# Scores of the two later query blocks as unpadded 64-row products of both halves in turn, in a hybrid encoder layer

## The chip, the cores and the metric

The kernel runs on one core of one Trainium2 chip. The metric is the device time of one execution in microseconds (us). Lower is better.

## What is computed

One layer of an encoder for 512 positions of width 1024. It has three parts in a row, each added to its input: a mixer (pooling, a recurrent time mixer called RWKV-7, and differential attention side by side, then an output projection), a cross-attention into 256 memory rows, and a gated feed-forward part. The change touches the differential attention alone. Cut to that:

```python
q, k, v = jnp.split(z, 3, axis=-1)                     # 4 heads, 2 halves of 64 features
q = rms_normalize(q.reshape(B, S, H, 2, 64)) * q_norm
k = rms_normalize(k.reshape(B, S, H, 2, 64)) * k_norm
def block(q_blk, start):                               # 4 blocks of 128 queries
    s = einsum('bqhcd,bkhcd->bhcqk', q_blk, k) * scale # a score matrix for each half c
    s = where(visible, s - slope * abs(qpos - kpos), -inf)
    p = softmax(s)
    p = p[:, :, 0] - lam * p[:, :, 1]
    return einsum('bhqk,bkhd->bqhd', p, v)
```

## The kernel before

Every large product is made of three products in a reduced float format (fp32r): each operand is held as a high part and a low part, and `mm3` (lines 330 to 333) adds high x high, high x low and low x high into one PSUM tile. So a product of `mm3` shows in a profile as one row each of L331, L332 and L333. Products that are not split (transposes with the identity, the small products of the recurrence) run in plain float32; each of them shows as two matmul records.

The program is written as a list of steps. A string, `MIX`, names the order of the steps of the mixer, and a scheduler that works with a timeline of its own decides the final order on each engine. It prefers what it takes to be ready first. So two products that stand next to each other in the source need not stand next to each other on TensorE.

The differential attention has the steps `q` (transposes of queries and keys of a head into `qk` and `qz`), `s` (`diff_s(h, i)`: scores and softmax of head `h`, query block `i`), `o` (`diff_o`: transposes `pT` and products with the values) and `n` (`diff_norm`). Because a block sees no later keys, block `i` needs `n = 128 (i + 1)` keys: 128, 256, 384 and 512 columns. A head has two halves `c` of 64 features. They lie in partitions 0 to 63 and 64 to 127 of `qk`. Before the change a half is picked out by padding: the stationary operand `qz[c]` holds the queries of half `c` in its 64 rows and zeros in the other 64 (lines 713 to 717), and the product runs over all 128 rows. In each block half 0 has its three products, then half 1. Its score tiles `S` come from the PSUM buffers `pr` for head 0 and `b` for the other heads, two buffers each. VectorE reduces a score tile with the bias (L750), and so frees it; ScalarE takes the exponential.

The kernel already has products over 64 rows elsewhere, in plain float32. The products `ua` (L476) and `uw` (L487) use one half of the rows. The products `T` (L575) use rows 0 to 63 for one PSUM tile and rows 64 to 127 for another. In the first quarter of `T` the scheduler put the two tiles one after the other; in the second they stand in turn (`T_706`, `T_707`, `T_706`, `T_707`, ...); in the third they begin with two of the same tile (`T_734`, `T_734`, `T_735`, `T_735`, then in turn). Other engines that the prediction speaks of: `ss` (L788, a column sum in `diff_norm`), the powers on GpSimd (`s_r` L680, `m_rstd` L402), and the recurrence of `chunk` (products `U` L905 and `S` L916, and the VectorE addition `r` L907).

Of the kernel before, what the change touches and what calls it, by code (L numbers as in the profile page):

```python
# [16 lines left out]
P = 128  # L17
S = 512
# [175 lines left out]
def trunk_body(ctx: ExitStack, tc: tile.TileContext, A):  # L194
# [11 lines left out]
    def slot(tag, bufs, shape=(P, 512), dt=F32, nm=None):  # L206
        cnt[0] += 1
        pool = keep if tag in ("d", "t", "r", "rb") else sb
        return pool.tile(list(shape), dt, name=f"{nm or tag}_{cnt[0]}", tag=tag, bufs=bufs)
# [10 lines left out]
    def rs(dt=F32, shape=(P, 512)):  # L220
        return slot("r", TB["r"], shape, dt)

    def ts(dt=F32, shape=(P, 512)):
        return slot("t", TB["t"], shape, dt)
# [7 lines left out]
    def kvs(dt=F32, shape=(P, 512)):  # L232
        return slot("kv", TB["kv"], shape, dt)

    def small(role, shape, bufs=4):
        return slot("s_" + role, bufs, shape)

    def ps(tag, nm=None):
        cnt[0] += 1
        if tag in ("a0", "a1"):  # L240
            return pp.tile([P, 512], F32, name=f"{nm or 'ps'}_{cnt[0]}", tag=tag, bufs=1)
        return pp.tile([P, 512], F32, name=f"{nm or 'ps'}_{cnt[0]}", tag=tag, bufs=2)

    def pr(nm=None):
        return ps("pr", nm)
# [5 lines left out]
    V, G, ACT, PE = nc.vector, nc.gpsimd, nc.scalar, nc.tensor  # L251
    mm = PE.matmul
# [72 lines left out]
    def act_el(*a, **k):  # L325

        with tc.issue_after(pre_el[0]):
            el_ins.append(ACT.activation(*a, **k).ins)

    def mm3(out, lh, ll, rh, rl, start, stop):  # L330
        mm(out, lh, rh, start=start, stop=False)  # L331
        mm(out, lh, rl, start=False, stop=False)  # L332
        mm(out, ll, rh, start=False, stop=stop)  # L333
# [139 lines left out]
    for p in range(2):  # L473
# [3 lines left out]
        a = rs()  # L477
# [6 lines left out]
    for p in range(2):  # L484
# [3 lines left out]
        s = kvs()  # L488
# [114 lines left out]
    for q in range(4):  # L603
        pt = pr("W0")
        p4 = pt.rearrange("p (c h v) -> p c h v", c=2, h=4)
        for c in range(2):
            for h in range(H):
                mm(p4[0:64, c, h, :], tav(2 * q + c, h)[64:128], AV[q][64:128, c, h, :],  # L608
                   start=True, stop=True)
# [84 lines left out]
    bias = slot("bias", 1)  # L694
# [11 lines left out]
    for h in range(H):  # L706
# [6 lines left out]
    qz = [[sb.tile([P, 512], F32R, name=f"qz{c}{i}", tag=f"qz{c}{i}", bufs=1) for i in range(2)]  # L713
          for c in range(2)]
# [24 lines left out]
    def diff_s(h, i):  # L739

        qk = qks[h]
        n = P * (i + 1)
        nmx, Z, rz = small("nmx", (P, 2)), small("Z", (P, 2)), small("rz", (P, 2))
        sc = []
        for c in range(2):
            st = pr("S") if h == 0 else ps("b", "S")
            qs = slice(i * P, (i + 1) * P)
            mm3(st[:, 0:n], qz[c][0][:, qs], qz[c][1][:, qs], qk[0][:, 0:n], qk[1][:, 0:n], True, True)
            s = ts()
            V.tensor_tensor_reduce(s[:, 0:n], st[:, 0:n], bias[:, 384 - P * i:S],  # L750
                                   -(0.25 ** (h + 1)), 3e38, ALU.add, ALU.min, nmx[:, c:c + 1])
            sc.append(s)
        for c in range(2):
            act_el(sc[c][:, 0:n], sc[c][:, 0:n], AF.Exp, scale=-1.0, bias=nmx[:, c:c + 1],
                   accum_out=Z[:, c:c + 1])
        V.reciprocal(rz, Z)
        V.tensor_scalar(rz[:, 1:2], rz[:, 1:2], lam, None, ALU.mult)
        if i >= 2:
            ACT.activation(sc[1][:, 0:n], sc[1][:, 0:n], AF.Copy, scale=rz[:, 1:2])
        else:  # L760
            V.tensor_scalar(sc[1][:, 0:n], sc[1][:, 0:n], rz[:, 1:2], None, ALU.mult)
        V.scalar_tensor_tensor(sc[0][:, 0:n], sc[0][:, 0:n], rz[:, 0:1], sc[1][:, 0:n],  # L762
                               ALU.mult, ALU.subtract)
        sc0[h, i] = sc[0]
# [275 lines left out]
    def v_rows(h):  # L1040
# [20 lines left out]
        "e": [lambda h=h: k_t(h) for h in range(H)],  # L1061
        "q": [lambda h=h: qks.update({h: qk_t(h)}) for h in range(H)],
        "s": [lambda h=h, i=i: diff_s(h, i) for h in range(H) for i in range(4)],
        "o": [lambda h=h, b=b: diff_o(h, *b) for h in range(H) for b in (((0, 1), (0, 1)), ((2, 3), (0, 1)), ((2, 3), (2, 3)))],
        "n": [lambda h=h: diff_norm(h) for h in range(H)],
# [52 lines left out]
    on, KT, Vm, qs, qr = {}, {}, {}, {}, {}  # L1118
# [354 lines left out]
```

## Time and profile before

| | us |
|---|---|
| median of 3 runs | 800.82 (800.76 to 801.9) |
| the profiled execution, its own time | 800.4 |
| its span, first to last instruction | 798.6 |
| TensorE busy in it | 785.8 (98%) |
| VectorE busy | 560.3 (70%) |
| ScalarE busy | 420.7 (53%) |

An engine's busy time is the time in which at least one of its instructions runs. Matmuls are pipelined, so their durations overlap: what one costs TensorE is read from the distance of two starts, not from its duration. The time outside the span (1.8 us) is start and end of the program.

### The profile page before, as it was taken

The numbers are of one execution on the slowest core, as the hardware profiler recorded it, in microseconds if no ns is written. First come the engines' busy times: TensorE is split into PE (matmuls) and PEld (weight loads), VectorE is DVE, ScalarE is ACT, GpSimd is POOL, SyncE is SP. The second block draws the span as 40 slices with busy tenths as digits, with TensorE's granted clock in tenths as the row PEclk, the third lists the DMA queues.
The fourth block names the chain that finished last, engine by engine and source line by source line (L and its number), as shares of the span: only waits on it lengthen the run. The fifth ranks groups of instructions, "written<-read, shape, count | busy, mean of one in ns | idle before, by whom it ended". The sixth has DMA issues, their size and how long they took to land.

```text
span 798.6 us, 11546 instructions
## 1 busy us (share of the span) xinstructions
PE 785.8 (98%) x4130; PEld 654.3 (82%) x4130; DVE 560.3 (70%) x1075; ACT 420.7 (53%) x778; POOL 64.0 (8%) x83
## 2 busy tenths in 40 slices
PE   8999999989899999999999999999999999999997
PEld 6867788879798888888888888888888888888886
DVE  6558668856798855756646576666666667898995
ACT  7364643576689854556545344444334344454662
POOL 3010400243600000000100000000000000000000
PEclk9999999989999999999999999999999999999999
DMA  7312113222021244221112322232222323534432
GB/s 268 132 67 92 67 54 132 80 81 80 27 92 57 79 149 154 93 81 66 40 66 80 123 90 100 86 103 93 93 96 89 106 93 124 183 115 131 132 94 79
DMA packets 43625, 79.22 MB, mean 99 GB/s; under 512 B 4784, under 2 KB 5936, under 8 KB 43568
## 3 DMA queue, kind: packets, MB, share of 16 engines
q1 hardware_dynamic: 41328, 75.35, 27.9%
q10 hardware_dynamic: 2240, 3.15, 1.2%
q8 instruction: 32, 0.52, 0.3%
q14 instruction: 25, 0.20, 0.1%
HBM read 76.38 MB, written 2.10 MB: 98 GB/s over the span
## 4 chain that ended last, share of the span: by engine, by line
PE 95%; ACT 1%; POOL 1%; issue 1%; DVE 1%; DMA 1%; DVEq 0%; SPq 0%; ACTq 0%
PE ps L331 23%; PE ps L333 22%; PE ps L332 22%; PE ps L1406 13%; POOL s_r L680 1%; PE T L575 1%; PE tr L523 1%; PE colsum L393 1%; PE S L332 1%; PE S L331 1%; PE S L333 1%; PE pT L775 1%; DMA wr<-in_wp_dram 1%; PE Sx L331 1%; PE W L608 1%
## 5 line engine op out<-in xcount | busy, mean ns | idle before, releaser
L174 ACT ACTIVATE wh<-wr 128x512 fp32r<-128x512 f32 x212 | 132.4, 628 | 159.3 <-PE ps L332 121.2
L175 DVE TENSOR_TENSOR wl<-wr,wh 128x512 fp32r<-128x512 f32 x212 | 146.0, 690 | 97.1 <-ACT wh L174 92.9
L331 PE MATMUL ps<-r,wh 128*128 128x512 f32 x416 | 162.3, 394 | 0.0
L332 PE MATMUL ps<-r,wh 128*128 128x512 f32 x416 | 162.0, 389 | 0.0
L333 PE MATMUL ps<-r,wl 128*128 128x512 f32 x416 | 161.2, 390 | 0.0
L333 PEld LDWEIGHTS ps<-r,wl 128*128 128x128 f32 x416 | 78.1, 188 | 16.5
L331 PEld LDWEIGHTS ps<-r,wh 128*128 128x128 f32 x416 | 78.1, 188 | 16.3 <-ACT r L312 0.2
L332 PEld LDWEIGHTS ps<-r,wh 128*128 128x128 f32 x416 | 78.2, 188 | 16.3 <-DVE t L762 0.2
L1406 PE MATMUL ps<-whid,ma 128*128 128x512 f32 x276 | 85.3, 389 | 0.0
L331 PE MATMUL ps<-wh,xh 128*128 128x256 f32 (+1 forms) x224 | 75.3, 336 | 0.2 <-ACT kv L1014 0.2
L332 PE MATMUL ps<-wl,xh 128*128 128x256 f32 (+1 forms) x224 | 74.9, 334 | 0.0
L1406 PEld LDWEIGHTS ps<-whid,ma 128*128 128x128 f32 x276 | 51.7, 188 | 11.2 <-ACT whid L312 0.5
L1406 PE MATMUL ps<-wlod,ma 128*128 128x512 f32 x138 | 53.4, 389 | 0.0
L312 ACT ACTIVATE whid<-r 128x512 fp32r<-128x512 f32 x55 | 34.3, 630 | 30.1 <-PE ps L1406 20.1
L1353 DVE TENSOR_TENSOR t<-ps,rb 128x512 f32<-128x512 f32 x44 | 29.4, 686 | 27.4 <-PE ps L333 27.0
L331 PEld LDWEIGHTS ps<-wh,xh 128*128 128x128 f32 x224 | 42.4, 189 | 5.4 <-issue 0.7
L332 PEld LDWEIGHTS ps<-wl,xh 128*128 128x128 f32 x224 | 42.5, 190 | 4.5 <-issue 0.7
L332 PE MATMUL ps<-xl,wh 128*128 128x512 f32 x112 | 44.2, 399 | 0.0
L313 DVE TENSOR_TENSOR wlod<-r,whid 128x512 fp32r<-128x512 f32 x55 | 36.8, 682 | 4.4 <-ACT whid L312 4.3
L332 PE MATMUL ps<-d,wh 128*128 128x512 f32 x96 | 37.7, 392 | 0.0
L333 PE MATMUL ps<-wh,xl 128*128 128x512 f32 x96 | 37.6, 393 | 0.0
L333 PE MATMUL ps<-d,wl 128*128 128x512 f32 x96 | 37.5, 390 | 0.0
(343 smaller groups left out, 1470.2 us busy)
## 6 DMA issues: line engine op xcount, KB each, us to landing
wr<-in_wp_dram SPq DMA_DIRECT2D x212, 256.0 KB, 2.6
r<-in_wd_dram SPq DMA_DIRECT2D x33, 256.0 KB, 2.7
wrawd<-in_wd_dram SPq DMA_DIRECT2D x22, 256.0 KB, 2.7
r<-in_xt_dram SPq DMA_DIRECT2D x8, 256.0 KB, 5.3
t<-in_xt_dram ACTq DMA_DIRECT2D x8, 256.0 KB, 2.7
out_dram<-t SPq DMA_DIRECT2D x8, 256.0 KB, 2.0
kv<-in_memt_dram ACTq DMA_DIRECT2D x4, 256.0 KB, 4.4
pm<-in_pmat_dram SPq DMA_DIRECT2D x1, 512.0 KB, 4.0
```

Source lines behind the costliest of these rows:

```text
L174: nc.scalar.activation(hi, raw, AF.Copy)
L175: nc.vector.tensor_tensor(lo, raw, hi.bitcast(F32), ALU.subtract)
L312: ins = ACT.activation(dhi, src, AF.Copy)
L313: V.tensor_tensor(dlo, src, dhi.bitcast(F32), ALU.subtract)
L331: mm(out, lh, rh, start=start, stop=False)
L332: mm(out, lh, rl, start=False, stop=False)
L333: mm(out, ll, rh, start=False, stop=stop)
L393: mm(pt[:, 2 * i:2 * i + 2], tot[:, i * P:(i + 1) * P], ones[:, 0:2], start=True, stop=True)
L523: PE.transpose(pv4[0:n, c, p, :], src(p, 2 * q + c), ident)
L575: mm(pts[hh].rearrange("p (c h t) -> p c h t", c=2, h=2)[:, c, p], KB[p][o:o + 64, cg, :], RA[p][o:o + 64, cg, :], start=True, stop=True)
L1353: V.tensor_tensor(dst[c], src[c], rb2, ALU.mult)
L1406: mm(X[p][tt], l, r, start=not onto and k == 0 and j == 0, stop=k == NG - 1 and j == 2, skip_group_check=onto)
```

## The change

For the blocks `i` = 2 and 3 of each head the padding is no longer multiplied. Half 0 uses rows 0 to 63 of both operands, half 1 rows 64 to 127. The source issues the six products of a block in turn: high x high of half 0, of half 1, then high x low of half 0, of half 1, then low x high. Both score tiles are taken before the first product. The zeros are still written, since blocks 0 and 1 still use them.

```diff
-        sc = []
+        sc, sts = [], [pr("S") if h == 0 else ps("b", "S") for _ in range(2)]
+        qs = slice(i * P, (i + 1) * P)
+        if i < 2:
+            for c in range(2):
+                mm3(sts[c][:, 0:n], qz[c][0][:, qs], qz[c][1][:, qs], qk[0][:, 0:n], qk[1][:, 0:n],
+                    True, True)
+        else:
+            for j, (a, b) in enumerate(((0, 0), (0, 1), (1, 0))):
+                for c in range(2):
+                    rows = slice(64 * c, 64 * c + 64)
+                    mm(sts[c][:, 0:n], qz[c][a][rows, qs], qk[b][rows, 0:n], start=j == 0, stop=j == 2)
         for c in range(2):
-            st = pr("S") if h == 0 else ps("b", "S")
-            qs = slice(i * P, (i + 1) * P)
-            mm3(st[:, 0:n], qz[c][0][:, qs], qz[c][1][:, qs], qk[0][:, 0:n], qk[1][:, 0:n], True, True)
             s = ts()
-            V.tensor_tensor_reduce(s[:, 0:n], st[:, 0:n], bias[:, 384 - P * i:S],
+            V.tensor_tensor_reduce(s[:, 0:n], sts[c][:, 0:n], bias[:, 384 - P * i:S],
```

The scheduler makes a new order of TensorE from it. These are three of the eight blocks. In the rows, `qz_866` and `qz_867` are the high and low part of half 0, `qz_868` and `qz_869` those of half 1; `ps` are products with weights, `pT` and `kT` transposes, `U`, `S_2055` and `y` products of the recurrence.

Head 1, block 2, on TensorE before:

```order
L905 MATMUL U_2049<-b_2036,at 128x128 x2
L1034 MATMUL kT_2590<-cs,kv_2152 128x128 x4
L331 MATMUL S_2237<-d_2075,qz_866 128x384
L332 MATMUL S_2237<-d_2076,qz_866 128x384
L333 MATMUL S_2237<-d_2075,qz_867 128x384
L331 MATMUL S_2243<-d_2075,qz_868 128x384
L332 MATMUL S_2243<-d_2076,qz_868 128x384
L333 MATMUL S_2243<-d_2075,qz_869 128x384
```

The same block in the changed kernel:

```order
L331 MATMUL ps_2630<-wh_1_2316,xh_1889 128x256
L754 MATMUL S_2237<-d_2075,qz_866 128x384
L754 MATMUL S_2237<-d_2076,qz_866 128x384
L754 MATMUL S_2237<-d_2075,qz_867 128x384
L754 MATMUL S_2238<-d_2075,qz_868 128x384
L754 MATMUL S_2238<-d_2076,qz_868 128x384
L754 MATMUL S_2238<-d_2075,qz_869 128x384
L923 MATMUL S_2055<-r_598,r_751 128x128 x2
```

The six products still stand side by side, but three of half 0 come first and then three of half 1. They moved behind a group of weight products.

Head 2, block 3, on TensorE before; the three products of its second half stand 23 rows further on, also side by side:

```order
L331 MATMUL o_2408<-p_2449,d_1300 128x256
L331 MATMUL S_2723<-d_2382,qz_866 128x512
L332 MATMUL S_2723<-d_2383,qz_866 128x512
L333 MATMUL S_2723<-d_2382,qz_867 128x512
L931 MATMUL y_2212<-r_774,r_599 128x128
```

The first half of this block in the changed kernel; its second half stands 10 rows further on, between weight products and the product `gnv`:

```order
L952 MATMUL gnm_2255<-r_1631,cs 128x512
L754 MATMUL S_2723<-d_2382,qz_866 128x512
L754 MATMUL S_2723<-d_2383,qz_866 128x512
L782 MATMUL pT_2599<-cs,t_2470 128x128 x2
L754 MATMUL S_2723<-d_2382,qz_867 128x512
L726 MATMUL qkT_2741<-cs,d_1937 128x128
```

The three products of one half are now in two pieces, with transposes over 128 rows between them.

Head 3, block 3, on TensorE before:

```order
L331 MATMUL ps_3248<-r_3002,wh_0_2964 128x512
L331 MATMUL S_3125<-d_2755,qz_866 128x512
L332 MATMUL S_3125<-d_2756,qz_866 128x512
L333 MATMUL S_3125<-d_2755,qz_867 128x512
L331 MATMUL S_3131<-d_2755,qz_868 128x512
L332 MATMUL S_3131<-d_2756,qz_868 128x512
L333 MATMUL S_3131<-d_2755,qz_869 128x512
L332 MATMUL ps_3248<-r_3003,wh_0_2964 128x512
```

The same block in the changed kernel:

```order
L333 MATMUL ps_3027<-wh_1_2934,xh_2021 128x256
L754 MATMUL S_3125<-d_2755,qz_866 128x512
L754 MATMUL S_3126<-d_2755,qz_868 128x512
L754 MATMUL S_3125<-d_2756,qz_866 128x512
L754 MATMUL S_3126<-d_2756,qz_868 128x512
L754 MATMUL S_3125<-d_2755,qz_867 128x512
L754 MATMUL S_3126<-d_2755,qz_869 128x512
L782 MATMUL pT_3144<-cs,t_2881 128x128
```

This is the one block of the eight in which the halves stand in turn. Around all of them rows of other steps changed places too, from the transposes of head 0 on to the first weight products of the output projection; behind these the order of TensorE is as before.

## Rows read from the trace of the kernel before

**Rows 1.** The page's first part: busy us (share of the span) and instructions.

```profile
PE 785.8 (98%) x4130; PEld 654.3 (82%) x4130; DVE 560.3 (70%) x1075; ACT 420.7 (53%) x778; POOL 64.0 (8%) x83
```

**Rows 2.** The page's chain that ended last, share of the span by engine.

```profile
PE 95%; ACT 1%; POOL 1%; issue 1%; DVE 1%; DMA 1%; DVEq 0%; SPq 0%; ACTq 0%
```

**Rows 3.** Windows of 10 us: us, PE, PEld, DVE, ACT, POOL busy, PE clock, DMA.

```profile
170.00:180.00 10.00, 8.96 (x95) 7.33 (x94) 6.99 (x21) 7.21 (x18) 8.51 (x13) 0.82 0.02 5
210.00:220.00 10.00, 7.47 (x46) 6.82 (x44) 8.39 (x28) 4.89 (x13) 4.29 (x6) 0.83 0.00 0
220.00:230.00 10.00, 10.00 (x80) 9.73 (x80) 9.41 (x31) 8.04 (x19) 0.00 (x0) 1.00 0.24 82
...
270.00:280.00 10.00, 10.00 (x52) 8.06 (x51) 8.62 (x20) 10.00 (x24) 0.00 (x0) 1.00 0.16 56
```

**Rows 4.** Timeline of PE, a block of 384 columns: start, duration, instruction.

```profile
265.79 0.34 PE L331 MATMUL S<-d,qz 128*128 128x384 f32 x1
...
266.83 0.28 PE L333 MATMUL ps<-wh,xh 128*128 128x256 f32 x1
```

**Rows 5.** Timeline of PE, a block of 512 columns.

```profile
270.84 0.39 PE L331 MATMUL S<-d,qz 128*128 128x512 f32 x1
...
272.23 0.39 PE L332 MATMUL ps<-r,wh 128*128 128x512 f32 x1
```

**Rows 6.** Timeline of PE around products over 64 rows, ua and uw.

```profile
43.21 1.98 PE L476 MATMUL ua<-r,pm 64*128 64x512 f32 x4
...
49.33 0.39 PE L333 MATMUL ps<-xh,wl 128*128 128x512 f32 x1
49.65 1.12 PE L487 MATMUL uw<-r,pm 64*128 64x512 f32 x2
50.70 0.50 PE L331 MATMUL ps<-xh,wh 128*128 128x512 f32 x1
51.04 0.40 PE L332 MATMUL ps<-xl,wh 128*128 128x512 f32 x1
```

**Rows 7.** Timeline of PE, first quarter of T: one half of the rows.

```profile
90.43 1.16 PE L575 MATMUL T<-b,b 64*128 64x128 f32 x8
91.51 0.50 PE L331 MATMUL ps<-wh,xh 128*128 128x512 f32 x1
```

**Rows 8.** Timeline of PE, second quarter of T: both halves in turn.

```profile
95.81 1.16 PE L575 MATMUL T<-b,b 64*128 64x128 f32 x16
96.90 0.50 PE L333 MATMUL ps<-wh,xl 128*128 128x512 f32 x1
```

**Rows 9.** Timeline of PE, third quarter of T: two, two, then in turn.

```profile
101.21 1.17 PE L575 MATMUL T<-b,b 64*128 64x128 f32 x16
102.31 0.95 PE L523 MATMUL tr<-cs,b 128*64 128x128 f32 x7
```

**Rows 10.** Timeline of PE, float32 over 128 rows between fp32r products.

```profile
124.58 0.60 PE L726 MATMUL qkT<-cs,d 128*128 128x128 f32 x4
124.93 0.48 PE L331 MATMUL ps<-xh,wh 128*128 128x512 f32 x1
125.25 0.39 PE L332 MATMUL ps<-xl,wh 128*128 128x512 f32 x1
```

**Rows 11.** Timeline of PE after head 0's last scores, and its longest wait.

```profile
176.91 0.44 PE L775 MATMUL pT<-cs,t 128*128 128x128 f32 x2
178.15 1.15 PE L840 MATMUL AT<-b,r 64*64 64x64 f32 x32 [0.79 <-DVE s_nmx L750]
...
213.55 0.71 PE L916 MATMUL S<-r,r 128*128 128x128 f32 x4 [2.04 <-DVE r L907]
```

**Rows 12.** Timeline of GpSimd before that wait.

```profile
202.40 8.24 POOL L680 TENSOR_TENSOR s_r<-s_ms,mhalf 128x8 f32<-128x8 f32 x4 [2.13 <-DVE s_ms L678]
...
211.17 1.14 POOL L402 TENSOR_TENSOR m_rstd<-m_ms,mhalf 128x2 f32<-128x2 f32 x1
```

**Rows 13.** Timeline of VectorE before that wait.

```profile
212.35 0.16 DVE L872 SCALAR_TENSOR_TENSOR rsm<-m_rstd 128x2 f32<-128x2 f32 x1 [0.59 <-POOL m_rstd L402]
```

## The prediction

> **What bounds the kernel now.** First the busy times and the chain that ended last: TensorE is busy for 785.8 of 798.6 us, and 95% of the chain is its own work [rows 1, 2]. Time that TensorE spends or saves goes to the end one for one, except where it waits anyway. Then the windows around the scores. From 220 to 280 us TensorE is busy without a gap in all six windows (the first and the last are shown), at full clock [rows 3]. Here lie the blocks of heads 1 to 3 that the change touches. The blocks of head 0 lie between 172 and 177 us, in a window with 1.0 us of idle time and a clock at half speed for part of it. A third place matters, 210 to 220 us: 2.5 us idle, again with a mean clock of 0.83, which is 3.4 of 10 us at the half of two levels. There TensorE waits 2.04 us for VectorE [rows 11].
>
> Then the timeline. Six products of 384 columns take 1.04 us from the first start to the start of what follows, 0.175 each [rows 4]. Six of 512 columns take 1.39, 0.23 each [rows 5]. The zeros cost nothing of their own: a product over 128 rows is paid by its columns. The change has 24 products of each size, so before they cost 24 x 0.175 + 24 x 0.23 = 9.7 us of TensorE.
>
> **What two halves in turn can give.** T shows it. Eight passes on one half of the rows take 1.08 us until the next product starts [rows 7]; sixteen, in both halves, take 1.09 [rows 8]. So two products in different halves of the rows share their time fully. The third quarter, whose order begins with two of one tile and then two of the other, also does sixteen in 1.10 [rows 9]. So they needn't alternate strictly; it is enough that they queue next to each other. I take it that three of half 0 followed by three of half 1 also share.
>
> The Trainium skill, page "TensorE: Matmul & The Clock Gate", section "The mechanism" of its part on packing, says that matmuls start and end strictly in program order. By that rule only the last product of half 0 would share with the first of half 1, and the sum below would be 0.35 us higher. [Rows 9] speak against the rule, and I go by the rows.
>
> **What changing between 128 and 64 rows costs.** This is the term that decides. Before `uw` a product of 512 columns takes 0.32 us until the next start instead of 0.23 (49.33 to 49.65). The two passes of `uw` then take 1.05 us (49.65 to 50.70). One pass is 0.43, since four are 0.86 longer than two [rows 6]. So 0.19 is too much. The first product over 128 rows behind takes 0.34 instead of 0.23 (50.70 to 51.04). Together 0.09 + 0.19 + 0.11 = 0.39 us for going in and coming out, or 0.195 for one change of the rows. T agrees: eight passes of 0.11 are 0.88, and 0.2 lies on top. It is not the change between float32 and fp32r: four transposes and the product behind them take 0.67 us (124.58 to 125.25), just the 4 x 0.11 + 0.23 that they take without a change [rows 10]. No row shows fp32r products over 64 rows. The bounds are 0 (the change of format without a change of rows) and 0.195. I take 0.195, since `uw`, `T` and what follows them show it on both sides, whatever the neighbour's format.
>
> **Counting in the new order.** The source puts the halves in turn, but the scheduler did so in one block of eight. As (head, block):
> - (1,2): one run of six, three and three: two changes of rows, 0.39, minus three shared products of 0.175: -0.13.
> - (1,3), (2,2), (3,2): two runs of three each, with products over 128 rows between them. Nothing is shared, four changes: +0.78 each.
> - (2,3): three runs (two, one, three): six changes, +1.17.
> - (3,3): one run in turn: 0.39 - 3 x 0.23 = -0.30.
>
> That is 22 changes of rows, 4.3 us, against 1.2 us shared: **+3.1 us**, all of it where TensorE has no gap.
>
> Head 0: (0,2) goes into a product over 32 rows and (0,3) comes out of it and ends in `AT` over 64 rows, which were changes before too. So three changes are new, 0.6 us, and (0,2) can share 0.5. Its second half waits for a free score tile, and TensorE waits 0.79 us behind these blocks anyway [rows 11]. I take **+0.1**.
>
> **Rows that moved.** Two are of a size to matter.
> - At 177 us the two transposes `pT` now stand ahead of the last three products of (0,3). These products were done before `pT`; now they wait for it. That is 0.7 us of work put behind, where TensorE waited 0.79 for VectorE's reduction of the first of these tiles. It cancels within 0.5.
> - `ss` now has 29 weight products behind it, until the transposes of head 1, instead of 8, and 7 products `U` fewer. A weight product has 256 columns, half of 0.23; a product `U` two passes of 64 columns, each half of T's 0.11. That makes 21 x 0.12 - 7 x 0.11 = 1.7 us earlier against TensorE's own work. Behind `ss` hangs a chain: ScalarE's squares, four powers on GpSimd (8.24 us), `m_rstd` until 212.3 [rows 12], and VectorE's `rsm`, behind which stands the addition that TensorE waits for [rows 13]. So of the 2.04 us up to 1.7 can go. But VectorE now does four small operations on the keys' statistics, each about as small as `rsm` (0.16), between `rsm` and that addition: 0.6 or more. Then it scales four tiles of keys ahead of the next reductions, on which the next scores wait. I take **0**, between -1.7 and +1.7 (one more half-speed stretch like the one there).
>
> Runs of `AT` and `U`: `AT` is cut into four instead of three, `U_306` into one instead of two. No difference.
>
> **Sum.** 800.4 + 3.1 + 0.1 = 803.6 us for the profiled execution. The median of the runs is 0.4 above it, so **804.0**, 0.4% slower.
>
> **Rivals.**
> - *The moved rows give the time back.* If the wait at 211 to 213 us goes (-1.7), and with it part of the half-speed stretch behind it, the change ends at 801 to 802. For it speaks that the chain on GpSimd is the only large wait left. Against it: VectorE's additional work in front of the same wait. It decides from about 1.6 us gained. Then the result is within 0.2%.
> - *Going into 64 rows costs nothing for fp32r*, so faster. Place: the 25 new changes. Then 1.7 us shared remain as a gain, 799.1. With 0.07 us for a change gain and loss are equal. Against it are [rows 6 to 9]; for it only that no fp32r product over 64 rows was seen. The page "TensorEngine Tiling (Array Packing)" of the Trainium skill, section "Theoretical Speedup", promises up to twice the speed for a contraction of 64. By that rule all 24 pairs would share, 4.8 us less; with eight runs of six and 16 changes (3.1 us) that too is -1.7 us, 799.1. The order excludes it: five blocks are apart.
> - *New waits.* The products that now stand right behind their producers (`S_1637` behind `AT`, the keys' transposes behind VectorE's scalings) stop TensorE, and its clock falls once more; a half-speed stretch of 3.4 us costs up to 1.7. Then 806 to 807. For it: VectorE is busy for 9.4 of 10 us at 220 to 230 [rows 3]. Against it: what is late for TensorE there would be late in a stretch that the change itself makes longer.
> - *No sharing of fp32r products*: +1.7, 805.7, within the range.
>
> **How the numbers follow.** Differences below 0.2% (1.6 us) can hardly be told from no change here. The forecast with its bounds, no sharing included, 802.4 to 806: 60%. Rows that give back, 800.0 to 802.4: 21%. No price, or more given back than I see, below 799.2: 12%. New waits, above 806: 7%. The range leaves out the fast rival and the worst of the waits: 800.2 to 806.5. Faster by over 0.2%: 0.12; within: 0.22; slower: 0.66, with the new waits in it.
>
> **What the profile after would show.** Each run of L754 among busy neighbours: 0.32 us (behind 512 columns) before its first product, 0.1 more before its second, and the same at its end. Three products of one half take three times the column price; in (1,2) and (3,3) six take the time of three. If the starts behind such a run stand at 0.175 or 0.23 without addition, the price is wrong. If six of (1,2) take more than four times 0.175 behind the entry, queued halves don't share. TensorE's idle time in the windows at 170 and 210 us (3.5 us before) tells what the moved rows did. The prediction fails if that idle time changes by over 2 us, or if the clock has a fall more or less.

## The result and the profile after

The changed kernel takes 808.0 us in the median of four runs (806.46 to 809.07), the kernel before, beside it, 800.79. The ratio is 1.0078, with a 95% interval of 1.0062 to 1.0094. So the change is slower, as predicted, but by 7 us and not by 3.2; 808.0 lies outside the predicted 800.2 to 806.5.

The profiled execution took 807.74 us with a span of 806.0, 7.4 more than before. This is the first part of the page, which answers to [rows 1]:

```profile
PE 792.9 (98%) x4130; PEld 655.4 (81%) x4130; DVE 560.2 (70%) x1075; ACT 421.7 (52%) x778; POOL 62.1 (8%) x83
```

TensorE is busy for 7.1 us more (785.8 before) and idle for 0.3 us more (13.1 against 12.8). So in this execution the loss is busy time, and the waits in sum are as before. Now the windows of the kernel after (us, then the busy time of PE, PEld, DVE, ACT and POOL, the granted clock, DMA), which answer to [rows 3]:

```profile
160.00:170.00 10.00, 7.14 (x74) 6.55 (x73) 3.27 (x12) 6.93 (x14) 0.00 (x0) 0.74 0.44 154
170.00:180.00 10.00, 9.68 (x59) 6.94 (x59) 7.17 (x19) 6.56 (x16) 8.20 (x13) 0.50 0.01 3
180.00:190.00 10.00, 10.00 (x90) 9.14 (x90) 4.54 (x11) 4.98 (x11) 6.41 (x11) 0.56 0.00 0
210.00:220.00 10.00, 9.25 (x75) 7.61 (x73) 9.03 (x25) 6.43 (x13) 6.40 (x6) 1.00 0.23 79
220.00:230.00 10.00, 9.78 (x72) 8.67 (x73) 9.52 (x34) 7.45 (x22) 0.62 (x1) 1.00 0.17 56
250.00:260.00 10.00, 8.78 (x51) 6.41 (x51) 7.22 (x15) 9.95 (x22) 0.00 (x0) 1.00 0.07 26
```

Two windows of the kernel before that were not shown yet:

```profile
160.00:170.00 10.00, 7.66 (x82) 7.14 (x81) 3.98 (x13) 7.70 (x15) 0.00 (x0) 0.84 0.47 158
180.00:190.00 10.00, 10.00 (x106) 9.56 (x105) 7.34 (x13) 6.53 (x14) 7.04 (x11) 1.00 0.16 54
```

The column to look at is the last but two, the clock. A window of 10 us with a clock of 0.74 has 5.2 us at the lower of its two levels (1.2 GHz in place of 2.4), since 1 - 0.52/2 is 0.74. After the change 5.2 + 10 + 8.8 us between 160 and 190 us are at half speed, **24.0 us in one piece**. Before it was 3.2 + 3.6 there and 3.4 at 214 us, 10.2 together. All this time TensorE is busy for 9.7 to 10 of 10 us from 170 us on: the same products take up to twice as long. The new order has also moved the waits: the 2.04 us at 213 us are gone (9.25 busy where it was 7.47). In their place are a new wait of 1.2 us at 256 us, for ScalarE's `d` (L315), and two smaller ones, 0.6 us at 232 and 0.3 at 220 us.

Now the rows' own price. Timeline of TensorE after: block (1,2), the first half of (1,3), block (3,3), and, behind the third "...", head 0 (start, duration, instruction, idle time before it).

```profile
224.00 0.28 PE L331 MATMUL ps<-wh,xh 128*128 128x256 f32 x1
224.21 0.80 PE L754 MATMUL S<-d,qz 64*128 64x384 f32 x6
224.94 0.71 PE L923 MATMUL S<-r,r 128*128 128x128 f32 x4
...
227.75 0.28 PE L332 MATMUL ps<-wl,xh 128*128 128x256 f32 x1
227.96 0.96 PE L754 MATMUL S<-d,qz 64*128 64x512 f32 x3
228.85 0.33 PE L782 MATMUL pT<-cs,t 128*128 128x128 f32 x1
...
277.32 0.28 PE L333 MATMUL ps<-wh,xh 128*128 128x256 f32 x1
277.53 0.96 PE L754 MATMUL S<-d,qz 64*128 64x512 f32 x6
278.42 0.66 PE L782 MATMUL pT<-cs,t 128*128 128x128 f32 x4
...
171.84 1.92 PE L754 MATMUL S<-d,qz 64*128 64x384 f32 x6
173.82 1.91 PE L821 MATMUL Y<-b,b 32*32 32x32 f32 x32
175.66 1.65 PE L754 MATMUL S<-d,qz 64*128 64x512 f32 x3
177.56 0.69 PE L782 MATMUL pT<-cs,t 128*128 128x128 f32 x2 [0.26 <-DVE t L769]
178.18 1.65 PE L754 MATMUL S<-d,qz 64*128 64x512 f32 x3
```

Six products of (3,3) take 0.89 us (277.53 to 278.42), as three of (1,3) do (227.96 to 228.85): two halves share their time. Block (1,2), three of one half and then three of the other, takes 0.73 instead of the 1.04 of [rows 4], so queued halves share as well; in the single starts of the trace its six stand in three pairs, 10 to 12 ns apart. The product ahead of a step into 64 rows takes 0.21 us to the next start (277.32 to 277.53), where it otherwise takes 0.12.

### The profile page after: what moved, and what is told of

It is laid out like the page before. It is cut to its first block, busy times and chain, and to the rows that moved or that the text cites. A ratio compares the mean times of both kernels' runs of the same rounds, so it can differ in the third digit from the quotient of the medians.

```text
span 806.0 us, 11544 instructions
## 1 busy us (share of the span) xinstructions
PE 792.9 (98%) x4130; PEld 655.4 (81%) x4130; DVE 560.2 (70%) x1075; ACT 421.7 (52%) x778; POOL 62.1 (8%) x83
## 3 DMA queue, kind: packets, MB, share of 16 engines
q10 hardware_dynamic: 2240, 3.15, 1.2%
## 4 chain that ended last, share of the span: by engine, by line
PE 94%; ACT 2%; DVE 2%; issue 1%; DMA 1%; DVEq 0%; SPq 0%; ACTq 0%
PE ps L331 22%; PE ps L333 22%; PE ps L332 22%; PE ps L1413 13%; PE S L754 1%; PE colsum L393 1%; PE T L575 1%; PE tr L523 1%; PE pT L782 1%; PE U L830 1%; DMA wr<-in_wp_dram 1%; PE Sx L331 0%; PE W L608 0%; PE Sx L333 0%; PE Sx L332 0%
## 5 line engine op out<-in xcount | busy, mean ns | idle before, releaser
L333 PE MATMUL ps<-wh,xh 128*128 128x256 f32 x128 | 37.9, 296 | 0.0
```

## The experiments

Each was timed beside the kernel before on the same chip (medians of before 801.4 to 801.7). "Order of before" and "order of after" mean that the order on every engine is the one of that kernel.

| | score products | order | median us | ratio, 95% | granted clock of the runs |
|---|---|---|---|---|---|
| e1 | 64 rows in heads 1 to 3 | before | 803.08 | 1.0021, 1.0010 to 1.0032 | 0.988 to 0.994 |
| e2 | 64 rows | before | 806.42 | 1.0063, 1.0045 to 1.0081 | 0.982 to 0.986 |
| e3 | 128 rows | after | 805.49 | 1.0047, 1.0027 to 1.0066 | 0.987 to 0.994 |
| e4 | 64 rows in head 0 | after | 806.23 | 1.0070, 1.0056 to 1.0084 | 0.984 to 0.985 |
| e6 | 128 rows, waits filled | before | 798.79 | 0.9967, 0.9953 to 0.9981 | 0.996 to 1.0 |
| e7 | 64 rows, waits filled | before | 803.21 | 1.0014, 1.0001 to 1.0027 | 0.993 to 0.996 |
| e8 | 64 rows in heads 1 to 3, in pairs | near before | 802.42 | 1.0013, 0.9999 to 1.0027 | 0.987 to 0.996 |
| e9 | 64 rows, waits filled | after | 806.46 | 1.0071, 1.0054 to 1.0087 | 0.992 to 0.994 |
| e10 | 64 rows in three blocks, waits filled | before | 798.31 | 0.9968, 0.9955 to 0.9982 | 0.995 to 1.0 |
| e12 | 128 rows, waits filled | after | 804.99 | 1.0036, 1.0023 to 1.0050 | 0.992 to 0.993 |

The clock of a run is its mean over the run. It changes from run to run: of the 73 runs of the kernel before beside these experiments, the 23 with 0.993 or more have a median of 800.53, the 31 with 0.989 or less 802.30.

**e1 and e4: the rows in one part of the heads.** The source of before, with the rows chosen in the loop; e4 has `h == 0`.

```diff
-            mm3(st[:, 0:n], qz[c][0][:, qs], qz[c][1][:, qs], qk[0][:, 0:n], qk[1][:, 0:n], True, True)
+            rows = slice(64 * c, 64 * c + 64) if i >= 2 and h > 0 else slice(0, P)
+            mm3(st[:, 0:n], qz[c][0][rows, qs], qz[c][1][rows, qs], qk[0][rows, 0:n], qk[1][rows, 0:n],
+                True, True)
```

> Rows 0 to 63 and 64 to 127 in heads 1 to 3 alone; head 0 keeps its padded products. The order on every engine is that of the kernel before. Counted by the prediction's own prices in that order (a change of rows 0.195 us, a shared product of 384 columns 0.175, of 512 columns 0.23): blocks (1,2) and (3,2) stand as one run of six, -0.13 each; (1,3), (2,2) and (2,3) as two runs of three, +0.78 each; (3,3) as one run of six, -0.30; in sum +1.8. Theory A (the prices are right, and what is too much in the changed kernel comes from the clock in head 0): 802.6 us, with half-speed stretches of 6.8 and 3.4 us as before. Rival B (the prices of the rows are too small, and they make the whole difference): 805 or more, with the clock as before. Rival C (the clock's long half-speed stretch comes and goes by chance, whatever the rows): a time that does not follow the count, between 800 and 806.

> 64 rows in head 0 alone, heads 1 to 3 padded; the order is that of the changed kernel but for four rows of block (3,3), which stand half by half. Theories A1 and A2 agree here: the time of the changed kernel less the 3.1 us that the rows of heads 1 to 3 were counted at, 804.9, with a half-speed stretch of some 24 us. Rival B (the prices are too small, and the clock costs little): 801 to 802. Rival C (chance): a short stretch as often as a long one.

e1 came out at +1.7 us for a count of +1.8, with a clock as before. So the prices of rows and sharing hold, and the rows of heads 1 to 3 don't make the whole loss. e4, without them, has the long half-speed stretch and most of the loss (1.0070). Its median is 1.3 us above the 804.9 expected. Its runs have a clock of 0.984 to 0.985, every time; the changed kernel's four have 0.985 to 0.987, and none of the kernel before is below 0.987. So the long stretch is not chance.

**e2 and e3: rows without the moves, moves without the rows.** Both are the changed source. For e2 a list holds the instruction numbers of each engine in the order of before, for e3 in the order of after, and ordering edges keep to it; e3 pads the products again.

```diff
+        for a, b in zip(row, row[1:]):
+            tc.add_manual_dep(known[f"I-{b}"], f"I-{a}", mybir.DependencyInfo(
+                mybir.DependencyClass.NoSync, mybir.DependencyReason.DATA), reason="forced order")
-                    rows = slice(64 * c, 64 * c + 64)
+                    rows = slice(0, P)
```

> The changed kernel with 64 rows in all eight blocks, but every engine is held in the order of the kernel before, by ordering edges without a wait. So the rows change and nothing moves. Without the clock it is +1.8 us for heads 1 to 3 and about +0.2 for head 0 (two new changes of rows, some sharing, and a wait of 0.79 us behind that takes up half a microsecond either way): 802.8. Theory A1 (the products over 64 rows in head 0 keep TensorE's clock at half speed): a stretch of 15 us or more that begins about 166 us, and 806 to 808. Theory A2 (the moved rows of head 0 keep it there): half-speed stretches of 6.8 and 3.4 us as before, 802.8. Rival C (chance): no tie of the stretch to either.

> The order of the changed kernel on every engine, held by ordering edges without a wait, but every score product padded over 128 rows as before. So things move and the rows don't change. Theory A1 (64 rows in head 0 keep the clock down): the clock rises by about 175 us, and what is left is what the moved rows do by themselves, in which the wait of 2.04 us at 213 us is gone: 799 to 801. Theory A2 (the moved rows keep it down): a half-speed stretch of some 24 us as in the changed kernel, 805. Rival C (chance): no tie of the stretch to either.

Windows of e2:

```profile
160.00:170.00 10.00, 7.37 (x77) 6.74 (x75) 3.24 (x11) 7.04 (x14) 0.44 (x1) 0.79 0.46 149
170.00:180.00 10.00, 9.94 (x85) 7.84 (x84) 6.88 (x22) 7.78 (x20) 9.07 (x16) 0.50 0.01 3
180.00:190.00 10.00, 10.00 (x93) 9.56 (x94) 5.94 (x11) 4.93 (x10) 5.92 (x8) 0.86 0.16 52
```

Windows of e3, and what TensorE waited for in it (total, times, longest):

```profile
170.00:180.00 10.00, 8.23 (x65) 7.09 (x64) 6.19 (x16) 5.39 (x14) 7.02 (x12) 0.67 0.08 31
180.00:190.00 10.00, 10.00 (x84) 8.51 (x84) 5.59 (x13) 6.07 (x13) 7.62 (x12) 0.59 0.01 2
```

```profile
PE pT L782 <- DVE t L769: 1.0, 1, 1.0
PE S L754 <- DVE s_nmx L757: 0.8, 1, 0.8
```

Nothing moved in e2, and its half-speed stretch is 17.0 us (4.2 + 10 + 2.8), where it was 6.8. This profiled execution is the fastest of its six runs (804.12, clock 0.986); four have 0.982, so their half-speed time is longer still. No run of e2 has a clock over 0.986, no run of before one below 0.987. So **64 rows in head 0 do keep the clock down**: e2 is 3.3 us slower than e1 (1.0063 against 1.0021), and head 0 is all that differs. But in e3 nothing has 64 rows that had 128, and it is slower by 3.8 us too, with 14.8 us at half speed between 170 and 190 us. There TensorE waits 0.8 and 1.0 us at the moved rows of block (0,3), in place of 0.79 in all [rows 11]. So A1 holds in e2, the moved rows cost time by themselves as well, and expecting 799 to 801 for e3 was wrong.

That the moved rows cost it through the clock, as A2 says, e3 does not show. Its half-speed time is in two pieces with full speed between them, not one of 24 us, and its profiled execution is the slowest of its eight runs (807.72). The clocks of the eight, 0.987 to 0.994, are those of the kernel before. Three with 0.991 or more have a median of 802.11, five with 0.989 or less 805.80. The runs of before on this chip have 800.75 and 802.33 in the same two groups. So at about the same clock, in few runs, the moved rows cost 1.4 and 3.5 us.

Both at once cost 5.6 (e4), not 7.1 (3.3 and 3.8). What fits is that at half speed TensorE comes later to `pT`: the wait there is 0.25 us in e4 and 0.26 in the changed kernel, where it is 1.0 in e3.

**e5 and e11: the clock by itself.** Two kernels of plain products, each executed once, in stretches that each begin behind a wait.

> Only a measurement: nothing of the layer is computed. Six stretches of products of 512 columns in fp32r, each behind a wait of some 12 us in which ScalarE copies and TensorE has nothing to do: 150 over 128 rows; 150 over rows 0 to 63 alone; 240 over 64 rows, the halves in turn; 150 over 128 rows with zeros in half of them; 100 over 128 rows, then 200 over rows 0 to 63, then 100 over 128 rows, without a wait; the same with 300 in turn in the middle. Theory A1 (products over 64 rows don't raise the clock): with 128 rows it rises within about 10 us of the start (the stretch of the kernel before was 6.8), with rows 0 to 63 it stays at half speed for the whole stretch, some 65 us; with zeros it rises as with 128 full rows. Whether two halves in turn raise it is open. A stronger form, A1b (they also pull it down): in the fifth stretch it falls in the middle. Rival D (the rows have nothing to do with the clock): it rises after the same time in all stretches. Prices: 0.23 us a product at full speed, two in turn 0.23 for both.

> Only a measurement: nothing of the layer is computed. Five stretches, each behind a wait of some 12 us, of products of 512 columns in fp32r. First, from half speed, groups of two over 128 rows and four over rows 0 to 63; second, groups of two and two; third, groups of three over rows 0 to 63 and three over rows 64 to 127. Theory A1 says for the third that it rises as two halves in turn did (5.7 us), if queued halves share; for the first and second it says only that they rise later than products over 128 rows alone or not at all. Fourth, from full speed, 700 float32 products of 32 x 32: theory A1 (small products count for less too): the clock falls in them; rival: it stays, since TensorE is busy. Fifth, the prices, at full speed: three over 128 rows and three over rows 0 to 63, 30 times: 6 x 0.23 + 0.39 = 1.77 us a group; three over 128 rows, three of one half and three of the other: also 1.77 if queued halves share, 2.46 if not; with the halves in turn 1.77.

Windows of e5: rows 0 to 63 alone; the first 6 us of two halves in turn; the same of 128 rows with zeros; rows 0 to 63 right behind 128 rows at full speed.

```profile
76.00:140.00 64.00, 63.97 (x150) 48.75 (x150) 0.00 (x0) 0.00 (x0) 0.00 (x0) 0.50 0.00 0
158.00:164.00 6.00, 5.96 (x30) 4.70 (x32) 0.00 (x0) 0.00 (x0) 0.00 (x0) 0.52 0.01 3
206.00:212.00 6.00, 6.00 (x15) 4.73 (x16) 0.00 (x0) 0.00 (x0) 0.00 (x0) 0.54 0.00 0
...
286.00:331.00 45.00, 45.00 (x199) 36.54 (x199) 0.00 (x0) 0.00 (x0) 0.00 (x0) 1.00 0.00 1
```

TensorE was busy for 63.97 of 64 us with one half of its rows, and the clock did not rise. With two halves in turn, or 128 rows half of them zeros, it was up within 6 us. Behind 128 rows at full speed the same one half kept full speed for 45 us. The Trainium skill, page "TensorE: Matmul & The Clock Gate", section "What's actually happening", says that the clock follows how busy TensorE has been, and that sustained activity releases it. The stretches of two halves in turn and of 128 rows agree with it; the 64 us of one half alone do not, and the measurement decides.

Windows of e11: groups of two over 128 and four over 64 rows of one half; three of one half and three of the other, behind their rise; 700 small products; then the three price stretches, 30 groups each.

```profile
21.45:210.72 189.27, 189.26 (x360) 99.22 (x360) 0.00 (x0) 0.00 (x0) 0.00 (x0) 1.00 0.00 0
...
435.00:459.80 24.80, 24.80 (x220) 20.87 (x216) 0.00 (x0) 0.00 (x0) 0.00 (x0) 1.00 0.01 1
...
497.00:566.00 69.00, 69.00 (x1298) 69.00 (x1297) 0.00 (x0) 0.00 (x0) 0.00 (x0) 0.50 0.01 2
624.62:677.91 53.29, 53.29 (x182) 28.82 (x180) 0.00 (x0) 0.00 (x0) 0.00 (x0) 1.00 0.00 0
677.91:731.76 53.85, 53.85 (x271) 29.40 (x270) 0.00 (x0) 0.00 (x0) 0.00 (x0) 1.00 0.00 1
731.76:785.50 53.74, 53.74 (x272) 29.11 (x270) 0.00 (x0) 0.00 (x0) 0.00 (x0) 1.00 0.00 1
```

In the first row the trace holds no record of the clock, and the column's 1.00 means nothing; the spacing tells it. Sixty groups of six take 189.27 us, 3.15 each, and six with one change in and out take 1.78 at full speed (53.29 / 30). Six at the spacing of the half-speed stretch of e5 (63.97 / 150 = 0.43) are 2.6. The spacing is the same from the first group to the last. So this stretch ran at half speed to its end, and so did the second (184.07 us for 40 groups, 4.60 where 8 x 0.23 + 2 x 0.39 is 2.62). The third, three and three, rose 4.8 us after its start. The small products brought the clock down, TensorE busy all the time. All this is as theory A1 said. The prices are 1.78, 1.80 and 1.79 us a group against 1.77 expected: a change in and out of 64 rows costs 0.40 us, and halves that are only queued behind each other share in full. The Trainium skill, page "TensorE: Matmul & The Clock Gate", section "The mechanism", has matmuls start and end strictly in program order. By that order the second price would be about 8 x 0.23 + 0.39 = 2.23, an estimate from the prices of this case; 1.80 was measured.

**e6 and e7: the waits filled.** Products on zeros, into PSUM tiles of their own: 3 ahead of the first scores of head 0, 5 and 4 ahead of two steps of the recurrence, 8 in the wait of 2.04 us. e6 has 128 rows, e7 has 64.

```diff
+            for _ in range(n):
+                mm(hold[-1], wz[:, 0:P], wz, start=True, stop=True)
```

> The kernel before (order and padding), with products on zeros, whose result nobody reads, put into four of TensorE's waits: 3 ahead of the first scores of head 0, 5 and 4 ahead of two steps of the recurrence behind them, and 8 into the wait of 2.04 us at 211 to 213 us. If the clock falls because of these waits, it now stays at full speed through 165 to 220 us: 10.2 us at half speed less, by the runs so far 0.28 us each, so 798.5 against 801.5, minus what the added products delay (up to 0.5 us). If the clock falls anyway, no gain: 801.5 to 802.

> The same added products, with 64 rows in all eight blocks in the order of the kernel before (so the kernel of e2 with its waits filled). Theory A1 (products over 64 rows only fail to raise a clock that has fallen): it does not fall, and the time is that of the run before plus the rows' own price of 1.2 to 2 us, about 800. Theory A1b (they pull it down themselves): a half-speed stretch of over 10 us remains, 803 to 806.

Windows of e6:

```profile
160.00:170.00 10.00, 9.19 (x94) 6.91 (x93) 4.44 (x13) 8.09 (x16) 0.00 (x0) 1.00 0.46 144
170.00:180.00 10.00, 8.48 (x93) 6.41 (x94) 8.11 (x22) 8.11 (x20) 9.51 (x15) 0.95 0.05 18
```

The second and third window of e7, and its timeline in the second:

```profile
170.00:180.00 10.00, 9.06 (x90) 6.75 (x88) 7.57 (x22) 7.92 (x20) 9.22 (x15) 0.70 0.06 21
180.00:190.00 10.00, 10.00 (x88) 9.56 (x89) 5.63 (x10) 4.52 (x9) 6.20 (x9) 0.79 0.14 52
```

```profile
171.52 1.38 PE L770 MATMUL S<-d,qz 64*128 64x384 f32 x6
172.97 1.25 PE L839 MATMUL Y<-b,b 32*32 32x32 f32 x32
174.15 2.39 PE L770 MATMUL S<-d,qz 64*128 64x512 f32 x6
```

In the kernel before the waits brought the clock down: with them filled it takes 2.9 us less (801.71 to 798.79; 798.5 expected). In e7 the filled waits give back 3.9 us of the 5.0 of e2 (ratios 1.0014 and 1.0063), but 803.2 is 3 us above the 800 of A1. The clock falls once more, for 10.2 us (0.70 and 0.79 in the two windows are 6.0 and 4.2 us), amid 64-row and 32-row products and with no wait of TensorE between 165 and 177 us. So beside small products the 64-row ones did not hold the clock, where the 128-row ones of e6 did up to 179 us (0.95 in its second window). Here it is A1b's forecast that came (over 10 us, 803 to 806). In e5 64-row products of 512 columns, with nothing between them, did hold it.

**e8: the pairs side by side.** The rows of e1; TensorE's list keeps the six of a block together and in turn.

```diff
+    six = [x for p in zip(A, B) for x in p]
+    row = rest[:j] + six + rest[j:]
```

> 64 rows in heads 1 to 3 alone, in the order of the kernel before on TensorE, but the six products of each block are held side by side and in turn (the first half of block (1,3) is moved back by seven products with weights, of block (2,2) by four small products; the other engines' order is the scheduler's). By the prediction's prices each block of 384 columns is then 0.39 - 3 x 0.175 = -0.13 us and each of 512 columns 0.39 - 3 x 0.23 = -0.30, in sum -1.3: 800.2 against 801.5. Rival: the scores that now stand later make VectorE, busy for 9.4 of 10 us there, late for what follows, and new waits give the gain back: 802 to 803.

Waits of TensorE in e8 that the kernel before does not have:

```profile
PE o L332 <- DVE p L313: 0.9, 1, 0.9
```

The median is 0.7 us above before, too little to be told from no change. In the profiled execution TensorE is idle for 1.3 us more (799.5 - 785.4 = 14.1 against 12.8), 0.9 of it behind VectorE's split of the probabilities `p`, as the rival said. It is busy for 0.4 us less, where the pairs were expected to save 1.3; why not more is open.

**e9 and e12: the order of after with its waits filled,** with 64 and with 128 rows: 4, 5 and 4 added products in the three early waits that e7 fills.

> The changed kernel, every engine held in its own order, with products on zeros (nobody reads them) put into three of its waits in head 0: 4 ahead of the first scores, 5 and 4 ahead of the two steps of the recurrence behind them. Theory A1 (the long half-speed stretch is the largest part of what was too much): it gets shorter by 9 to 14 us, as in e7 against e2, and the time falls from 808 to 803.5 to 805.5. Rival E (waits of the moved rows are the larger part, the clock little): 807 or more, whatever the clock does.

> The kernel of e3 (order of the changed kernel, all products over 128 rows) with the added products of e9 in the same three waits. It asks how much of the 3.8 us by which e3 was slower is the clock, and how much the waits that the moved rows bring with them. Theory F (waits: 1.6 us more idle time than before in e3's profile; the rest is the clock, which these waits bring down once more): with the clock mostly up the time is that of e6 plus 1.6 to 2.5, 800.4 to 801.3. Rival G (the moved rows cost as much with the clock up): e6 plus 3.8, 802.6 or more.

Timeline of e9 at the moved rows, its windows, then those of e12:

```profile
172.64 1.19 PE L839 MATMUL Y<-b,b 32*32 32x32 f32 x32
175.03 0.97 PE L770 MATMUL S<-d,qz 64*128 64x512 f32 x3 [1.19 <-DVE s_nmx L773]
176.97 0.69 PE L798 MATMUL pT<-cs,t 128*128 128x128 f32 x2 [0.96 <-DVE t L785]
```

```profile
170.00:180.00 10.00, 7.70 (x69) 5.20 (x71) 8.20 (x20) 7.16 (x18) 8.78 (x15) 0.83 0.04 13
180.00:190.00 10.00, 10.00 (x92) 9.07 (x89) 4.79 (x11) 4.98 (x10) 5.85 (x9) 0.66 0.02 7
```

```profile
170.00:180.00 10.00, 7.62 (x75) 5.53 (x74) 8.70 (x22) 7.05 (x19) 8.78 (x15) 0.81 0.02 5
180.00:190.00 10.00, 10.00 (x83) 9.19 (x84) 4.53 (x9) 4.49 (x9) 5.37 (x9) 0.68 0.07 25
```

Both expectations of e9 miss in the time. The half-speed stretch is 13.8 us shorter (3.4 + 6.8 = 10.2 in place of 24.0), as A1 said, and the clock of the runs is 0.992 to 0.994. But the time is 806.46, only 1.5 us below the changed kernel, and by the ratios (1.0071 and 1.0078) the two can't be told apart. With a faster TensorE the waits at (0,3) are 1.19 and 0.96 us, where the changed kernel waits 0.26. So in the new order the long half-speed stretch and these waits stand in for one another, and the clock alone doesn't explain the loss.

e12 has these waits too (1.3 and 1.0), and its clock falls there, for 3.8 + 6.4 = 10.2 us with not one 64-row score product in the program. It is 5.5 us slower than e6 (1.0036 against 0.9967), from which it differs in the order, in one product more in the first wait, and in the eight products in a wait that this order doesn't have. The time is in the range of rival G, but G's condition, the clock up, did not come. In the two profiled executions the 5.5 us of span are 2.6 us more idle time (12.8 against 10.2) and 2.7 more busy time (791.0 against 788.3), so a part is waiting, and the fallen clock can be the rest. With the early waits filled the moved rows cost no less than without.

**e10: what is left as a better version.** e6, with 64 rows in the blocks whose halves stand side by side in the order of before.

```diff
+PAIRED = ((1, 2), (3, 2), (3, 3))
-                    rows = slice(0, P)
+                    rows = slice(64 * c, 64 * c + 64) if (h, i) in PAIRED else slice(0, P)
```

> The kernel of e6 (order of before, waits filled), with 64 rows only in the three blocks whose two halves stand side by side in that order: (1,2), (3,2), (3,3). By the prices -0.13 - 0.13 - 0.30 = -0.56 on top of e6: 798.2. Rival: (1,2) shared only in part in e1, so -0.4 or less, which can't be told from e6: 798.4 to 798.8.

798.31 us, 0.32% below before, the expected 798.2; the rows' share of it can't be told from e6. Both are about 3 us faster than the kernel before.

## Why the prediction was wrong

- **TensorE is the bound:** right. The 7.4 us of span are 7.1 us of its busy time.
- **Price of a change of rows, and sharing:** right. From the single starts, the six blocks of heads 1 to 3 cost -0.12, +0.76, +0.73, +1.08, +0.79 and -0.34 us, **+2.9** in sum, where the prediction counted -0.13, +0.78, +0.78, +1.17, +0.78 and -0.30, +3.1. For (3,3): 0.89 - 6 x 0.23 = -0.49, and 0.09 and 0.06 at its two ends. e11 gives the price without the kernel around it. That queued halves share was shown in (1,2) and in e11. In whole runs the rows of heads 1 to 3 cost 1.7 us (e1, counted +1.8 in that order); between e4 and the changed kernel they are 0.6 us by the ratios and 1.8 by the medians, with intervals that overlap.
- **Head 0, +0.1:** this step failed. It counted changes of rows and sharing and took the clock as given. In the order of before these rows cost 3.3 us (e2 against e1), because the clock that has fallen among the waits at 164 to 169 us no longer rises at 173.6 us. In the trace of before it rises near the end of block (0,2), as the lines below show; [rows 3] gave 0.82 for that window. That the change takes rows from the very products in which the clock came back was not asked.
- **Rows that moved, 0 between -1.7 and +1.7:** this step failed too: they cost +3.8 us by themselves (e3). The gain that was priced did come, the wait at 213 us is gone, but the new waits at 220, 232 and 256 us, 2.1 us together, take it back: the waits in sum stay, but not for the reasons given. And around (0,3), of which the text said that it "cancels within 0.5", TensorE waits 0.8 us for VectorE's reductions and 1.0 us for the tile of the `pT` that moved ahead, wherever it gets there at a higher clock (e3, e9, e12). In the changed kernel itself the wait there is only 0.26 us, behind products at half speed.
- **The sum of both:** the profiled 7.4 us are 2.9 for the rows of heads 1 to 3, 0.3 of idle time, and 4.2 that are left, beside 13.8 us more at half speed (24.0 against 10.2). That the clock costs time in the order of before is shown by e2, e6 and e7. The 4.2 are a remainder: e9, with 13.8 us of the half speed gone, is at most 1.5 us faster, so they are not the price of the clock alone.
- **New waits and one more clock fall, 806 to 807 (7%):** the nearest rival in its number, and right that waits and the clock would make the loss. It looked for a new fall behind new waits at 220 us; there the clock stays at full speed. The stretch at 165 us lengthened, by 13.8 us and not 3.4. That 64 rows act on the clock stood in no rival.
- **"The prediction fails if that idle time changes by over 2 us, or if the clock has a fall more or less":** both came. The idle time in the windows at 170 and 210 us fell from 3.6 us to 1.1 (9.68 and 9.25 busy). And there is one fall fewer; the one left is 24 us long.

Timeline of TensorE before, the longest of the early waits, then where the clock rises in block (0,2): a product of 384 columns takes 0.32 us to the next start from 172.82 to 173.14, and 0.26 from 173.74 to 174.00.

```profile
166.31 1.58 PE L814 MATMUL Y<-b,b 32*32 32x32 f32 x32 [1.04 <-DVE s_nmx L750]
...
172.82 0.52 PE L333 MATMUL S<-d,qz 128*128 128x384 f32 x1
173.14 0.52 PE L331 MATMUL S<-d,qz 128*128 128x384 f32 x1
...
173.74 0.34 PE L333 MATMUL S<-d,qz 128*128 128x384 f32 x1
174.00 1.19 PE L814 MATMUL Y<-b,b 32*32 32x32 f32 x32
```

Open stays why the scheduler makes another order. How the 3.8 us of the moved rows divide between their waits and the clock was not separated either: in e3's profiled execution TensorE is idle for 1.8 us more than before (805.9 - 791.3 = 14.6), and filling the earlier waits made these longer.

## What to carry to other kernels

A column price holds only at the clock at which it was read. Where a stretch lies near a half-speed one, ask behind which products the clock comes back, and whether the change takes rows from them. Unpadding to 64 rows gains where both halves are queued side by side, six products in a run (-0.1 to -0.3 us here); alone each run costs 0.4. Waits near the lower clock can be worth filling: in the order of before 20 products that nobody reads were worth 2.9 us, more than any version of the change. In the order of after 13 of them gave back at most 1.5 us: there other waits took the place of the slow products.

## What the hardware showed

- Products of one half of the rows, TensorE busy throughout, left the clock at half speed for 64 us (e5), and groups of two full and four half ones for 189 us (e11). With two halves in pairs it rose within 6 us, as with 128 rows half of them zeros. At full speed one half alone kept it for 45 us (e5).
- Among 32 x 32 float32 products it fell, TensorE busy all the while (e11).
- Three products of rows 0 to 63 and then three of rows 64 to 127 ran in three pairs, 10 to 12 ns apart in block (1,2): a queue of two halves need not be written in turn.
- A change into 64 rows and out again costs 0.40 to 0.42 us at full speed in e11, and 0.36 to 0.40 for each run of one half in the changed kernel.
